# The first two merge gates of the delta-rule branch computed as one pair of column blocks, with seven block products in three of eight k-tile pairs

## The chip, the cores and the metric

The kernel runs on one core of one Trainium2 chip. The metric is the device time in microseconds, as a median over repeated runs. TensorE (PE) does the matrix products, PEld is its weight load, VectorE is DVE, ScalarE is ACT, GpSimd is POOL, and SP issues the loads of the weights.

## What is computed

One layer of a hybrid decoder trunk, in float32, for 256 tokens of width 2048:

```python
xn = _rmsnorm(h, norm_mix_g[i])
z = xn @ w_in[i]
zm, zr, zs, zg = jnp.split(z, IN_SPLIT, axis=-1)
...
g_m, g_r, g_s = jnp.split(jax.nn.sigmoid(zg), N_BRANCH, axis=-1)
mixed = (g_m * (y_m @ w_up_m[i]) + g_r * (y_r @ w_up_r[i]) + g_s * (y_s @ w_up_s[i]))
h = h + mixed @ w_out[i]
hn = _rmsnorm(h, norm_ffn_g[i])
h = h + (jax.nn.silu(hn @ ffn_w_gate[i]) * (hn @ ffn_w_up[i])) @ ffn_w_down[i]
hp = _rmsnorm(h, norm_ple_g[i])
h = h + (p[i] @ ple_w_proj[i]) * jax.nn.sigmoid(hp @ ple_w_gate[i])
return _rmsnorm(h, final_norm_g)
```

`y_r` is the delta-rule branch (RWKV-7), `g_r` its merge gate: a product of the 256 x 2048 activations with 2048 of the columns of `w_in`.

## The kernel before, in words

Every float32 operand of a large product is split into a high and a low part (`hi`, `lo`), and a product is three matmuls: high by high, low by high, high by low (`mm2`, lines 142 to 148). The tokens are two halves of 128 (`TS`). The activations stand in `ahi` and `alo`, 16 k-tiles of 128 each. The weights lie in HBM as chunks of 1 MB, in the order in which they are used. A chunk holds four tiles of 128 x 512. SP loads it into one of three `raw` buffers; ACT casts it into `whi` and DVE subtracts to get `wlo` (lines 131 and 132 in `chunk`), two tiles at a time, with three buffers each for `whi` and `wlo`.

`gemm_tm` multiplies 16 k-tiles with a block of 512 columns: four chunks, 96 matmuls of 512 columns, into two PSUM banks, one for each half of the tokens. PSUM has eight banks here, in two pools of four: `mm` (through `pmm()`) for the large products and `sm` (through `psm()`) for everything else.

`gemm_pair` does two blocks of 512 columns at once, in eight steps over pairs of k-tiles. It takes all four `mm` banks. An ordinary step is a chunk with four tiles and eight block products, 24 matmuls. A step of `SEVEN` is a Strassen-Winograd step: four sums of weight tiles (`seven`: two by POOL at lines 241 and 245, two by DVE), seven tiles to split, seven block products, 21 matmuls. Four of its seven products go to banks of `sm`, which the pair holds from the first such step to the last:

```python
if u == by7[0]:
    for q in (1, 7, 5, 6):
        M[q] = psm("M%d" % q)
(b11, b21), (b22, t3), (t1, t2_), (t4_,) = seven(pool)
...
prods([(1, A(u, 0, 0), b11)], end)
prods([(2, A(u, 0, 1), b21)], last)
prods([(3, S(u, 3), b22)], last)
prods([(7, S(u, 2), t3)], end)
```

Before the change it is used in the feed-forward part alone, with `ORDER = (3, 4, 0, 5, 1, 6, 2, 7)` and `SEVEN = (0, 1, 2)` for the gate and up blocks.

The order of instructions on each engine is made by a planner when the program is built: it takes what it expects to be ready, by priority, which is the order in the text, except for what stands under `tc.high_priority()`. So large products fill PE while the chain of the delta rule goes on. That chain stands in the text ahead of the gates of S5 and of the delta rule: `rw_chunk(0)` to `rw_chunk(3)`, then `rw_norm`. All its matmuls write `sm` banks. `rw_chunk` writes `pu` and `py` (lines 1130 and 1136), copies `pu` to `Up`, multiplies it into `px` (line 1148), copies that to `UV`, and finishes `py` (line 1136). `rw_norm` normalises `Yr` (DVE, ACT, and a power on POOL at line 1179), makes the bonus term in two banks `pq` (line 1185), and transposes `Yr` into two banks `pt` (line 1192). Then come the S5 gates and up blocks, the four delta-rule gates `z_gate("r", n)`, and the four up blocks of `y_r`.

Of the kernel before, what the change touches and what calls it, by code (L numbers as in the profile page):

```python
# [37 lines left out]
ORDER = (3, 4, 0, 5, 1, 6, 2, 7)  # L38
SEVEN = (0, 1, 2)

DORDER = tuple(range(22))
DSEVEN = (5, 8, 11, 14, 17)
# [35 lines left out]
def trunk(ctx: ExitStack, tc: tile.TileContext, xT, x, pT, wall, vecs, csts, s5b, s5c, gfin, out, dbg=None):  # L78
# [78 lines left out]
    TS = [slice(t * 128, (t + 1) * 128) for t in range(2)]  # L157
# [32 lines left out]
    def split(hi, lo, src, gain=None):  # L190

        if gain is None:
            nc.scalar.copy(out=hi, in_=src)  # L193
            nc.vector.tensor_tensor(out=lo, in0=src, in1=hi.bitcast(F32), op=ALU.subtract)  # L194
        else:
            nc.scalar.activation(out=hi, in_=src, func=AF.Identity if not isinstance(gain, float) else AF.Copy, scale=gain)
            nc.vector.scalar_tensor_tensor(out=lo, in0=src, scalar=gain, in1=hi.bitcast(F32), op0=ALU.mult, op1=ALU.subtract)
# [14 lines left out]
        tt(sf[:, 2], a[:, 0, TS[0]], a[:, 0, TS[1]], ALU.subtract)  # L212
        tt(sf[:, 3], a[:, 1, TS[0]], sf[:, 1], ALU.subtract)

    def sums_of(hi, lo, u, pool, tag="s"):

        af = t2("af").rearrange("p (a t) -> p a t", a=2)
        sf = t2("sf").rearrange("p (a t) -> p a t", a=4)
        tt(af, hi[:, 2 * u:2 * u + 2, :].bitcast(F32), lo[:, 2 * u:2 * u + 2, :].bitcast(F32), ALU.add)
        sums(sf, af)  # L220
        r = tuple(pool.tile([128, 4, 128], F32R, name=q + "%d" % u, tag="%s%s%d" % (tag, q, u)) for q in ("h", "l"))
        split(*r, sf)
        return r

    def tiled(r):

# [3 lines left out]
        split(hi, lo, r)  # L230
        return [(hi[:, q], lo[:, q]) for q in range(n)]

    def seven(pool):

        if not loaded:
            load()
        raw, _ = loaded.pop(0)
        with tc.high_priority():
            ts_ = pool.tile([128, 3, 512], F32, name="tsum", tag="tsum", bufs=2)
            out_ = [tiled(raw[:, 0:2])]  # L240
            nc.gpsimd.tensor_tensor(out=ts_[:, 0], in0=raw[:, 3], in1=raw[:, 0], op=ALU.subtract)  # L241
            tt(raw[:, 3], raw[:, 2], raw[:, 3], ALU.subtract)
            out_.append(tiled(raw[:, 2:4]))
            tt(ts_[:, 1], raw[:, 3], raw[:, 0], ALU.add)
            nc.gpsimd.tensor_tensor(out=ts_[:, 2], in0=raw[:, 1], in1=ts_[:, 1], op=ALU.subtract)
            out_ += [tiled(ts_[:, 0:2]), tiled(ts_[:, 2:3])]
        return out_
# [5 lines left out]
        while late:  # L253
            late.pop(0)()

    def gemm_pair(A, S, order, by7, pool, prep=None, onto=None):

        M = {q: pmm() for q in (2, 4, 3, 8)}
        done, res = set(), None

        def prods(ops, last):

            n_ = {q: max(i for i, o in enumerate(ops) if o[0] == q) for q in {o[0] for o in ops}}
            for part in range(2):
                for i, (q, a, w) in enumerate(ops):
                    mm2(M[q], *a, *w, part, q not in done, last and part == 1 and i == n_[q], True)
                    if part == 0:
                        done.add(q)

        for i, u in enumerate(order):  # L270
            if i == 2:
                run_late()
            last = u == order[-1]
            if prep is not None:
                prep(u)
            if u in by7:
                if u == by7[0]:
                    for q in (1, 7, 5, 6):
                        M[q] = psm("M%d" % q)
                (b11, b21), (b22, t3), (t1, t2_), (t4_,) = seven(pool)  # L280
                end = u == by7[-1]
                prods([(1, A(u, 0, 0), b11)], end)
                prods([(2, A(u, 0, 1), b21)], last)
                prods([(3, S(u, 3), b22)], last)
                prods([(7, S(u, 2), t3)], end)
                prods([(5, S(u, 0), t1)], end)
                prods([(6, S(u, 1), t2_)], end)
                prods([(4, A(u, 1, 1), t4_)], last)
                if end:

                    with tc.high_priority():
                        m1, u2, u3, u4, v4 = (t2(q) for q in ("m1s", "u2", "u3", "u4", "v4"))
                        nc.scalar.copy(out=m1, in_=M[1])
                        tt(u2, M[6], m1, ALU.add)
                        tt(u3, M[7], u2, ALU.add)
                        tt(u4, M[5], u2, ALU.add)
                        tt(v4, M[5], u3, ALU.add)
                    res = (m1, u3, u4, v4)
                    if onto is not None:
                        for o, r in zip(onto, res):  # L300
# [30 lines left out]
    def tt(o, a, b, op):  # L331
        nc.vector.tensor_tensor(out=o, in0=a, in1=b, op=op)
# [32 lines left out]
    ahi = act.tile([128, NKT, T], F32R, name="ahi", tag="ahi")  # L365
# [115 lines left out]
    G = {}  # L481
# [362 lines left out]
    mixed, gates = {}, {}  # L844

    def z_gate(key, n):
        ps = gemm_tm(xh, xl, NKT)
        with tc.high_priority():
            for t in range(2):
                g_ = t2("gate")  # L850
                act_fn(g_, ps[t], AF.Tanh, scale=hrs0[:, t:t + 1])
                gates[key, t, n] = g_

    def up(key, n, hi, lo, nkt, first):
        ps = gemm_tm(hi, lo, nkt)
        with tc.high_priority():
            for t in range(2):
                g_ = gates.pop((key, t, n))
                stt(g_, g_, 1.0, ps[t], ALU.add, ALU.mult)
                if first:  # L860
                    mixed[t, n] = g_
                else:
                    tt(mixed[t, n], mixed[t, n], g_, ALU.add)
# [387 lines left out]
    for n in range(4):  # L1251
        z_gate("s", n)
        up("s", n, lambda k: G["ysh"][:, k, :], lambda k: G["ysl"][:, k, :], 4, False)
    for n in range(4):
        z_gate("r", n)
    mT = {}
    for n in range(4):
# [53 lines left out]
    gu = gu_stack.enter_context(tc.tile_pool(name="gu", bufs=1))  # L1311
    hh, hl = hT

    SF = {u: sums_of(hh, hl, u, gu) for u in SEVEN}

    def A(u, t, k):
        return hh[:, 2 * u + k, TS[t]], hl[:, 2 * u + k, TS[t]]

    for b in range(11):
        c11, c21, c12, c22 = gemm_pair(A, lambda u, i: tuple(q[:, i, :] for q in SF[u]), ORDER, SEVEN, hid_p)  # L1320

        def swiglu(b=b, c11=c11, c21=c21, c12=c12, c22=c22):
            sg = []
            for t, (g_, u_) in enumerate(((c11, c12), (c21, c22))):
                s_ = t2("sg")
                act_fn(s_, g_, AF.Silu, scale=rs1[:, t:t + 1])
                stt(s_, u_, rs1[:, t:t + 1], s_, ALU.mult, ALU.mult)
                sg.append(s_)
            for q in range(4):
                pt = psm()  # L1330
                for t in range(2):
                    nc.tensor.transpose(pt[:, t * 128:(t + 1) * 128], sg[t][:, q * 128:(q + 1) * 128], ident)  # L1332
                nc.scalar.copy(out=hid[:, 4 * b + q, :], in_=pt[:, 0:T])
        late.append(swiglu)
# [24 lines left out]

    for n in (0, 2):  # L1360
        gemm_pair(lambda u, t, k: tuple(q[:, k, TS[t]] for q in dv["a"]), lambda u, i: tuple(q[:, i, :] for q in dv["s"]),
                  DORDER, DSEVEN, hid_p, down_prep, (h[0, n], h[1, n], h[0, n + 1], h[1, n + 1]))
        late.append(lambda n=n: [h_block(m, hT2, "gple", ssq2) for m in (n, n + 1)])
        if n == 0:
            late.append(p_halves)
# [74 lines left out]
def layout(i):  # L1440
# [35 lines left out]
    def block(w):  # L1476
        k = w.shape[0]
        for c in range(k // 512):
            chunks.append(w[c * 512:(c + 1) * 512].reshape(4, 128, 512).transpose(1, 0, 2).reshape(128, 2048))

    def blocks(w):
        for n in range(w.shape[1] // 512):
            block(w[:, n * 512:(n + 1) * 512])

    block(w_in[:, 6088:6600])
    block(lora_c)
    blocks(w_in[:, 0:4096])
# [9 lines left out]
    for n in range(4):  # L1497
        block(w_in[:, 10696 + n * 512:10696 + (n + 1) * 512])
        block(a["w_up_s"][0][:, n * 512:(n + 1) * 512])
    blocks(w_in[:, 8648:10696])  # L1500
    blocks(a["w_up_r"][0])
    blocks(a["w_out"][0])

    def pair(l, r, order):

        l, r = (q.reshape(-1, 2, 128, 512) for q in (l, r))
        for u in order:
            chunks.append(np.stack([l[u, 0], l[u, 1], r[u, 1], r[u, 0]], axis=1).reshape(128, 2048))

    for n in range(11):  # L1510
        c = slice(n * 512, (n + 1) * 512)
# [50 lines left out]
```

## Time and profile before

| | |
|---|---|
| median of 3 runs | 1658.6 us (1657.91 to 1659.91) |
| the profiled execution | 1657.76 us |
| its span in the profile | 1655.9 us |
| PE busy | 1633.6 us (99%) |
| DVE busy | 1314.9 us (79%) |
| ACT busy | 912.9 us (55%) |
| POOL busy | 202.7 us (12%) |

The span runs from the first to the last instruction; 1.86 us of the profiled execution lie around it. A busy PE is a pipelined one: matmuls overlap, so that the distance from one to the next is shorter than the duration of one.

### The profile page before, as it was taken

The page shows a single profiled execution, that of the slowest core. Times are in us where ns is not written, and L with a number is a line of the kernel's source. Part 1 is how long each engine was busy: PE and PEld are TensorE (multiplying, and loading weights), DVE is VectorE, ACT ScalarE, POOL GpSimd, SP SyncE. Part 2 cuts the span into 40 slices and gives each one's busy share as a digit, 9 for nine tenths or more (in the row PEclk, how much of TensorE's full clock was granted, in tenths as well). Part 3 has the DMA queues.
Part 4 walks back from the last instruction along what each step waited for, and adds up shares of the span by engine and source line. Part 5 has one row for each costly group of instructions (what it writes and reads, how often), then busy time and mean ns, then how long its engine had stood idle before and what let it go on. Part 6 is the DMA issues. An engine that isn't in the chain of part 4 may idle for free. (4 is left out here: it accounts for less than half of the span.)

```text
span 1655.9 us, 23640 instructions
## 1 busy us (share of the span) xinstructions
PE 1633.6 (99%) x9225; PEld 1375.7 (83%) x9225; DVE 1314.9 (79%) x1672; ACT 912.9 (55%) x1174; POOL 202.7 (12%) x151
## 2 busy tenths in 40 slices
PE   8999999999999999999999999999999999999997
PEld 8999889987888878888887888888888888888886
DVE  6999776969988546565588889899888988888665
ACT  6465466555645443444556555555555566666554
POOL 1100100100000000000032222222222121011000
PEclk9999999999999999999999999999999999999999
DMA  9654545555454444555544555455555555555553
GB/s 364 198 171 174 174 153 177 196 187 182 175 181 156 149 156 155 189 196 193 203 175 181 204 203 194 191 192 189 201 204 203 189 193 203 198 199 196 226 189 116
DMA packets 49456, 313.70 MB, mean 189 GB/s; under 512 B 5824, under 2 KB 9152, under 8 KB 12736
## 3 DMA queue, kind: packets, MB, share of 16 engines
q1 hardware_dynamic: 43488, 304.59, 50.8%
q0 software_dynamic: 3840, 3.15, 1.0%
q10 hardware_dynamic: 2016, 4.46, 0.8%
q8 instruction: 72, 1.18, 0.3%
q14 instruction: 40, 0.33, 0.1%
HBM read 306.93 MB, written 2.10 MB: 187 GB/s over the span
## 5 line engine op out<-in xcount | busy, mean ns | idle before, releaser
L131 ACT CAST whi<-raw 128x1024 fp32r<-128x1024 f32 (+1 forms) x476 | 495.7, 1048 | 492.2 <-PE mm L146 336.5
L132 DVE TENSOR_TENSOR wlo<-raw,whi 128x1024 fp32r<-128x1024 f32 (+1 forms) x476 | 602.4, 1271 | 192.2 <-ACT whi L131 166.7
L146 PE MATMUL mm<-whi,alo 128*128 128x512 f32 x512 | 201.5, 394 | 0.0
L145 PE MATMUL mm<-whi,ahi 128*128 128x512 f32 x512 | 201.2, 393 | 0.0
L145 PE MATMUL mm<-whi,hhi 128*128 128x512 f32 x506 | 199.5, 394 | 0.5 <-ACT whi L193 0.2
L146 PE MATMUL mm<-whi,hlo 128*128 128x512 f32 x506 | 197.1, 390 | 0.0
L152 PE MATMUL mm<-ahi,whi 128*128 128x256 f32 x576 | 143.2, 286 | 7.4 <-ACT whi L131 7.4
L148 PE MATMUL mm<-wlo,hhi 128*128 128x512 f32 x506 | 146.3, 393 | 2.2 <-DVE wlo L194 2.0
L153 PE MATMUL mm<-alo,whi 128*128 128x256 f32 x576 | 142.7, 286 | 0.0
L148 PE MATMUL mm<-wlo,ahi 128*128 128x512 f32 x512 | 139.3, 393 | 0.0
L241 POOL TENSOR_TENSOR tsum<-raw 128x512 f32<-128x512 f32 x43 | 66.3, 1542 | 551.1 <-DMA raw<-in_wall 269.4
L193 ACT CAST whi<-raw 128x1024 fp32r<-128x1024 f32 x86 | 90.4, 1051 | 66.8 <-PE mm L146 52.7
L194 DVE TENSOR_TENSOR wlo<-raw,whi 128x1024 fp32r<-128x1024 f32 x86 | 119.1, 1405 | 6.9 <-PE mm L148 6.5
L152 PEld LDWEIGHTS mm<-ahi,whi 128*128 128x128 f32 x576 | 111.4, 194 | 8.3 <-ACT whi L131 7.4
L145 PEld LDWEIGHTS mm<-whi,hhi 128*128 128x128 f32 x506 | 95.1, 188 | 24.5 <-issue 3.9
L148 PEld LDWEIGHTS mm<-wlo,hhi 128*128 128x128 f32 x506 | 94.7, 188 | 24.0 <-DVE wlo L194 4.5
L145 PE MATMUL mm<-whi,dh 128*128 128x512 f32 x292 | 114.0, 392 | 0.0
L145 PEld LDWEIGHTS mm<-whi,ahi 128*128 128x128 f32 x512 | 96.2, 188 | 21.1 <-issue 1.2
L146 PEld LDWEIGHTS mm<-whi,alo 128*128 128x128 f32 x512 | 96.3, 188 | 20.9 <-issue 1.2
L146 PE MATMUL mm<-whi,dl 128*128 128x512 f32 x292 | 113.5, 390 | 0.0
L148 PEld LDWEIGHTS mm<-wlo,ahi 128*128 128x128 f32 x512 | 95.7, 188 | 20.5 <-issue 0.4
L153 PEld LDWEIGHTS mm<-alo,whi 128*128 128x128 f32 x576 | 111.4, 194 | 0.7 <-issue 0.4
(558 smaller groups left out, 2935.7 us busy)
## 6 DMA issues: line engine op xcount, KB each, us to landing
raw<-in_wall SPq DMA_DIRECT2D x283, 1024.0 KB, 4.8
xrow<-in_x SPq DMA_DIRECT2D x2, 1024.0 KB, 9.3
h<-in_x ACTq DMA_DIRECT2D x8, 256.0 KB, 3.1
xraw<-in_xT SPq DMA_DIRECT2D x3, 512.0 KB, 9.5
ub<-Bh POOLq DMA_DIRECT2D x16, 64.0 KB, 3.9
ub<-uh POOLq DMA_DIRECT2D x16, 64.0 KB, 3.8
gft<-in_gfin ACTq DMA_DIRECT2D x1, 1024.0 KB, 7.4
out_dram<-fin SPq DMA_DIRECT2D x4, 256.0 KB, 3.2
```

Source lines behind the costliest of these rows:

```text
L131: nc.scalar.copy(out=hi[:, q, :], in_=r)
L132: nc.vector.tensor_tensor(out=lo[:, q, :], in0=r, in1=hi[:, q, :].bitcast(F32), op=ALU.subtract)
L145: nc.tensor.matmul(ps, ah, wh, start=first, stop=False, skip_group_check=skip)
L146: nc.tensor.matmul(ps, al, wh, start=False, stop=False, skip_group_check=skip)
L148: nc.tensor.matmul(ps, ah, wl, start=False, stop=last, skip_group_check=skip)
L152: nc.tensor.matmul(ps, wh, ah, start=first, stop=False, skip_group_check=skip)
L153: nc.tensor.matmul(ps, wh, al, start=False, stop=False, skip_group_check=skip)
L193: nc.scalar.copy(out=hi, in_=src)
L194: nc.vector.tensor_tensor(out=lo, in0=src, in1=hi.bitcast(F32), op=ALU.subtract)
L241: nc.gpsimd.tensor_tensor(out=ts_[:, 0], in0=raw[:, 3], in1=raw[:, 0], op=ALU.subtract)
```

## The change

The blocks 0 and 1 of the delta-rule gates are computed by one `gemm_pair` (`z_gate2`); blocks 2 and 3 and the up blocks stay as they were. The sums of the activations that the three steps of seven products need (`sums_of`) are made for it too; they take the room of tiles that `rw_inverse` has left (`Dm`, `cm`, `X`, `XT`, `Y`, and one of the small buffers `b2`). The sums of weights take a buffer of `b8`, a pool of two, which `KR` and `UV` hold until the delta rule's last chunk. The weights of the two blocks are laid out in HBM by pairs. The tanh of the gates is taken from SBUF instead of PSUM. In the feed-forward part the same functions are called through other names.

```diff
-    def sums_of(hi, lo, u, pool, tag="s"):
+    def sums_of(hi, lo, room):
 
         af = t2("af").rearrange("p (a t) -> p a t", a=2)
         sf = t2("sf").rearrange("p (a t) -> p a t", a=4)
-        tt(af, hi[:, 2 * u:2 * u + 2, :].bitcast(F32), lo[:, 2 * u:2 * u + 2, :].bitcast(F32), ALU.add)
+        tt(af, hi.bitcast(F32), lo.bitcast(F32), ALU.add)
         sums(sf, af)
-        r = tuple(pool.tile([128, 4, 128], F32R, name=q + "%d" % u, tag="%s%s%d" % (tag, q, u)) for q in ("h", "l"))
-        split(*r, sf)
-        return r
+        split(*room, sf)
+        return room
+
+    def room_pb(i):
+        t_ = [G["pb"].tile([128, 512], F32, name="sx", tag=q) if q else t2("sx") for q in (("Dm", "cm"), ("X", "XT"), ("Y", None))[i]]
+        return tuple(q.rearrange("p (a t) -> p a t", a=4).bitcast(F32R) for q in t_)
+
+    def tsum_t8():
+        return t8("tsum").rearrange("p a t -> p (a t)")[:, 0:1536].rearrange("p (a t) -> p a t", a=3)
...
+    def act_of(hi, lo):
+        return lambda u, t, k: (hi[:, 2 * u + k, TS[t]], lo[:, 2 * u + k, TS[t]])
+
+    def sum_of(sf):
+        return lambda u, i: tuple(q[:, i, :] for q in sf[u])
...
+    def z_gate2(key, n, sf):
+
+        c4 = gemm_pair(act_of(ahi, alo), sum_of(sf), ORDER, SEVEN, tsum_t8)
+        with tc.high_priority():
+            for o, (t, m) in zip(c4, ((0, n), (1, n), (0, n + 1), (1, n + 1))):
+                act_fn(o, o, AF.Tanh, scale=hrs0[:, t:t + 1])
+                gates[key, t, m] = o
...
-    for n in range(4):
+    z_gate2("r", 0, {u: sums_of(ahi[:, 2 * u:2 * u + 2, :], alo[:, 2 * u:2 * u + 2, :], room_pb(u)) for u in SEVEN})
+    for n in (2, 3):
         z_gate("r", n)
...
-    blocks(w_in[:, 8648:10696])
+    pair(w_in[:, 8648:9160], w_in[:, 9160:9672], ORDER)
+    blocks(w_in[:, 9672:10696])
```

## Rows read from the trace of the kernel before

**Rows 1.** The page, busy time of PE: us, share of the span, instructions.
```profile
PE 1633.6 (99%) x9225; PEld 1375.7 (83%) x9225; DVE 1314.9 (79%) x1672; ACT 912.9 (55%) x1174; POOL 202.7 (12%) x151
```

**Rows 2.** What PE waited for: us in total, times, longest.
```profile
PE mm L152 <- ACT whi L131: 7.4, 1, 7.4
PE mm L148 <- DVE wlo L194: 2.0, 3, 1.5
```

**Rows 3.** Windows: us; busy PE, PEld, DVE, ACT, POOL; PEclk; DMA share; GB/s.
```profile
620.93:650.70 29.77, 29.77 (x219) 23.67 (x218) 17.34 (x21) 10.76 (x14) 0.00 (x0) 1.00 0.39 136
650.70:674.60 23.90, 23.90 (x161) 19.81 (x160) 16.00 (x15) 12.44 (x16) 3.79 (x1) 1.00 0.50 177
674.60:696.40 21.80, 21.80 (x98) 18.06 (x97) 9.80 (x8) 9.63 (x12) 0.00 (x0) 1.00 0.56 198
```

**Rows 4.** The bonus product's operand and matmuls by tile: ns, first and last start us.
```profile
L1185 PE MATMUL sm<-mur,ct x8: 379/380/484, 639.3 to 640.9; 128*128 128x256 f32 x8
...
L335 DVE SCALAR_TENSOR_TENSOR mur<-mur,vt,muk x4: 480/480/486, 500.8 to 502.0; 128x256 f32<-128x256 f32 x4
```

**Rows 5.** Timeline: the delta rule between its first two chunks: start us, us.
```profile
588.21 0.37 ACT L1165 COPY Yr<-sm 128x256 f32<-128x256 f32 x1 [2.34 <-PE sm L1136]
...
594.00 1.15 PE L1130 MATMUL sm<-ST,KR 64*64 64x64 f32 x32
```

**Rows 6.** An earlier case by tile: mLSTM scores, an S5 slice, mLSTM numerators.
```profile
L335 DVE SCALAR_TENSOR_TENSOR E<-sm,E x4: 552/558/558, 179.1 to 184.9; 128x384 f32<-128x384 f32 x4
...
L611 PE MATMUL sm<-ub x8: 280/283/366, 184.6 to 201.7; 96*128 96x256 f32 x8
...
L807 PE MATMUL sm<-vtm,E x2: 379/380/382, 201.8 to 202.0; 128*128 128x258 f32 x2
```

**Rows 7.** Timeline: the delta rule's last chunk and its norm, on four engines.
```profile
633.79 0.37 ACT L1144 COPY Up<-sm 128x256 f32<-128x256 f32 x1 [2.42 <-PE sm L1136]
...
638.68 0.68 PE L1148 MATMUL sm<-Up,NX 64*64 64x64 f32 x16
...
640.00 0.43 DVE L1150 COPY UV<-sm 64x256 f32<-64x256 f32 x1
...
644.19 0.33 PE L1136 MATMUL sm<-UV,GB 128*64 128x64 f32 x2
...
649.86 1.29 DVE L332 TENSOR_TENSOR bon<-sm,muv 128x512 f32<-128x512 f32 x2
...
652.19 1.22 DVE L132 TENSOR_TENSOR wlo<-raw,whi 128x1024 fp32r<-128x1024 f32 x1
...
653.72 3.79 POOL L1179 TENSOR_TENSOR grs<-st,nhalf 128x16 f32<-128x16 f32 x1 [135.10 <-ACT whi L131]
...
657.54 1.23 DVE L332 TENSOR_TENSOR Yr<-Yr,grs 128x1024 f32<-128x1024 f32 x1
...
663.17 2.08 PE L1192 MATMUL sm<-ct,Yr 64*64 64x64 f32 x64
```

**Rows 8.** Groups of the pairs in the feed-forward part, and one tile's first and last start.
```profile
L194 DVE TENSOR_TENSOR wlo<-raw,whi 128x1024 fp32r<-128x1024 f32 x86 | 119.1, 1405 | 6.9 <-PE mm L148 6.5
...
L194 DVE TENSOR_TENSOR wlo<-tsum,whi 128x1024 fp32r<-128x1024 f32 x86 | 90.1, 1057 | 26.0 <-PE mm L148 16.2 <-PE sm L1332 7.0 <-ACT whi L193 0.6
...
L332 DVE TENSOR_TENSOR raw<-raw 128x512 f32<-128x512 f32 x43 | 29.5, 686 | 26.0 <-POOL tsum L241 26.0
...
L332 DVE TENSOR_TENSOR m1s<-mm,m1s x11: 680/682/684, 877.5 to 1308.4; 128x512 f32<-128x512 f32 x11
```

**Rows 9.** Timeline: PE's first matmuls, after its wait at the start.
```profile
9.71 0.42 PE L152 MATMUL mm<-ahi,whi 128*128 128x256 f32 x1
9.92 0.41 PE L153 MATMUL mm<-alo,whi 128*128 128x256 f32 x1
...
10.45 0.28 PE L152 MATMUL mm<-ahi,whi 128*128 128x256 f32 x1
10.57 0.28 PE L153 MATMUL mm<-alo,whi 128*128 128x256 f32 x1
```

More of the change, by code (lines that the diff above doesn't have):

```diff
@@ L213, in sums, with room_of, tsum_of @@
         tt(sf[:, 3], a[:, 1, TS[0]], sf[:, 1], ALU.subtract)
-    def sums_of(hi, lo, u, pool, tag="s"):
+    def sums_of(hi, lo, room):
         af = t2("af").rearrange("p (a t) -> p a t", a=2)
         sf = t2("sf").rearrange("p (a t) -> p a t", a=4)
-        tt(af, hi[:, 2 * u:2 * u + 2, :].bitcast(F32), lo[:, 2 * u:2 * u + 2, :].bitcast(F32), ALU.add)
+        tt(af, hi.bitcast(F32), lo.bitcast(F32), ALU.add)
         sums(sf, af)
-        r = tuple(pool.tile([128, 4, 128], F32R, name=q + "%d" % u, tag="%s%s%d" % (tag, q, u)) for q in ("h", "l"))
-        split(*r, sf)
-        return r
+        split(*room, sf)
+        return room
+    def room_of(pool, name):
+        return tuple(pool.tile([128, 4, 128], F32R, name=name + q) for q in ("h", "l"))
+    def room_pb(i):
+        t_ = [G["pb"].tile([128, 512], F32, name="sx", tag=q) if q else t2("sx") for q in (("Dm", "cm"), ("X", "XT"), ("Y", None))[i]]
+        return tuple(q.rearrange("p (a t) -> p a t", a=4).bitcast(F32R) for q in t_)
+    def tsum_of(pool):
+        return lambda: pool.tile([128, 3, 512], F32, name="tsum", tag="tsum", bufs=2)
+    def tsum_t8():
+        return t8("tsum").rearrange("p a t -> p (a t)")[:, 0:1536].rearrange("p (a t) -> p a t", a=3)
     def tiled(r):
@@ L231, in tiled, with seven @@
         return [(hi[:, q], lo[:, q]) for q in range(n)]
-    def seven(pool):
+    def seven(room):
         if not loaded:
@@ L238, in seven @@
         with tc.high_priority():
-            ts_ = pool.tile([128, 3, 512], F32, name="tsum", tag="tsum", bufs=2)
+            ts_ = room()
             out_ = [tiled(raw[:, 0:2])]
@@ L254, in run_late, with gemm_pair @@
             late.pop(0)()
-    def gemm_pair(A, S, order, by7, pool, prep=None, onto=None):
+    def act_of(hi, lo):
+        return lambda u, t, k: (hi[:, 2 * u + k, TS[t]], lo[:, 2 * u + k, TS[t]])
+    def sum_of(sf):
+        return lambda u, i: tuple(q[:, i, :] for q in sf[u])
+    def gemm_pair(A, S, order, by7, room, prep=None, onto=None):
         M = {q: pmm() for q in (2, 4, 3, 8)}
@@ L279, in gemm_pair @@
                         M[q] = psm("M%d" % q)
-                (b11, b21), (b22, t3), (t1, t2_), (t4_,) = seven(pool)
+                (b11, b21), (b22, t3), (t1, t2_), (t4_,) = seven(room)
                 end = u == by7[-1]
@@ L1312, in trunk @@
     hh, hl = hT
-    SF = {u: sums_of(hh, hl, u, gu) for u in SEVEN}
-    def A(u, t, k):
-        return hh[:, 2 * u + k, TS[t]], hl[:, 2 * u + k, TS[t]]
+    SF = {u: sums_of(hh[:, 2 * u:2 * u + 2, :], hl[:, 2 * u:2 * u + 2, :], room_of(gu, "sf%d" % u)) for u in SEVEN}
     for b in range(11):
-        c11, c21, c12, c22 = gemm_pair(A, lambda u, i: tuple(q[:, i, :] for q in SF[u]), ORDER, SEVEN, hid_p)
+        c11, c21, c12, c22 = gemm_pair(act_of(hh, hl), sum_of(SF), ORDER, SEVEN, tsum_of(hid_p))
         def swiglu(b=b, c11=c11, c21=c21, c12=c12, c22=c22):
@@ L1361, in trunk @@
         gemm_pair(lambda u, t, k: tuple(q[:, k, TS[t]] for q in dv["a"]), lambda u, i: tuple(q[:, i, :] for q in dv["s"]),
-                  DORDER, DSEVEN, hid_p, down_prep, (h[0, n], h[1, n], h[0, n + 1], h[1, n + 1]))
+                  DORDER, DSEVEN, tsum_of(hid_p), down_prep, (h[0, n], h[1, n], h[0, n + 1], h[1, n + 1]))
         late.append(lambda n=n: [h_block(m, hT2, "gple", ssq2) for m in (n, n + 1)])
@@ L1483, in blocks, with pair @@
             block(w[:, n * 512:(n + 1) * 512])
+    def pair(l, r, order):
+        l, r = (q.reshape(-1, 2, 128, 512) for q in (l, r))
+        for u in order:
+            chunks.append(np.stack([l[u, 0], l[u, 1], r[u, 1], r[u, 0]], axis=1).reshape(128, 2048))
     block(w_in[:, 6088:6600])
@@ L1499, in layout @@
         block(a["w_up_s"][0][:, n * 512:(n + 1) * 512])
-    blocks(w_in[:, 8648:10696])
+    pair(w_in[:, 8648:9160], w_in[:, 9160:9672], ORDER)
+    blocks(w_in[:, 9672:10696])
     blocks(a["w_up_r"][0])
     blocks(a["w_out"][0])
[L1504 to L1508, printed above, removed]
     for n in range(11):
```

## The prediction

> **What bounds the kernel now.** I read the page's busy time first: PE is busy for 1633.6 of 1655.9 us [rows 1]. The list of waits tells what that is worth: PE waits 7.4 us once, at the start, and after that hardly at all, 2.0 us in three waits being the next entry [rows 2]. So a matmul less is time less, and a microsecond in which PE stands still is a microsecond more; nothing behind it can give it back.
>
> Next the windows around the change. The third block of the four gates (674.60 to 696.40) is undisturbed: 21.80 us for 96 matmuls, 0.227 us each [rows 3]. The first block takes 29.77 us and the second 23.90, since matmuls of the delta rule run between theirs: 8.0 and 2.1 us more than 21.8 [rows 3]. That is the point that matters: the gates are the filling of PE while the last chunks of the delta rule and its norm go on.
>
> Last the timelines of that chain, with one question: who gets the banks of `sm`? The bonus product's operand is finished by 502.5 us, but its matmuls run at 639.3 [rows 4], right behind the last chunk's `px`, which starts at 638.68 [rows 7]. Nor did it lack a bank: between 588.6 us, when a chunk's results are copied out, and 594.0, when the next chunk begins, the chunk's new state alone can hold one of the four [rows 5]. In the text it stands behind `px`. An earlier case looks the same: the numerators' first operand is finished by about 179.7, yet their first matmul runs at 201.8, right behind the S5 slice that stands ahead of them in the text and was late [rows 6]. I read both as one rule of this planner: a tile of a pool gets no buffer before all tiles that come ahead of it in the text have theirs, even if buffers are free.
>
> **The change part by part.** *Removed.* The pair has 5 x 24 + 3 x 21 = 183 matmuls in place of 192: nine times 0.227 = 2.0 us less on PE.
>
> *Moved behind the norm.* The pair's four products M1, M7, M5 and M6 go to `sm`. In the text they come behind `rw_norm`, whose last two banks are those of the transposes at line 1192. By the rule above M1 can't begin before these transposes have; they start at 663.17 [rows 7]. The old gates, in `mm` alone, knew no such tie. The pair reaches M1 far earlier. It starts at 620.93 and has before M1 two ordinary steps, 48 matmuls or 10.9 us, and then the products 2 and 3 of the first step of seven, 6 matmuls or 1.4 us. Nothing else can fill PE: `whi` and `wlo` have three buffers, the first holds the tile of product 1, the second and third those of products 7, 5 and 6, so neither the seventh tile nor the next step's get a place; the blocks 2 and 3 need `mm` banks, and the pair has all four. PE can do the delta rule's own matmuls, 8.0 + 2.1 = 10.1 us [rows 3]. In all 22.4 us of work until M1.
>
> When do the transposes come, with PE idle? From the chain as it was [rows 7], step by step. `Up` is copied by 634.16, `px` starts at 638.68: 4.5 us, because PE had its queue full of gate matmuls. Now PE runs out of ordinary work at about 635.5 (620.93 + 10.9, and some 3.7 of the delta rule's 8.0): 3.2 us earlier. `UV` is written by 640.43, and the next product starts at 644.19, 3.8 us later. Now it waits only for the bonus product, about 2 us behind `px`, which leaves 0.9 us: 2.8 us less. Then DVE put the bonus multiply and a weight split (1.29 us at 649.86, 1.22 us at 652.19) between the norm's steps, together some 2.2 us. The first is out of the way by then, the second has no buffer to write: 2.2 us less. The power on POOL, 3.79 us, stays. From the end of the last multiply, 658.77, to 663.17 are again 4.4 us of queue; now about 0.1: 4.3 less. Sum 12.5, so the transposes start at 650.7 and end, 2.08 us later, at 652.8. From 620.93 that is 31.9 us, less 22.4 of work: PE stands still for 9.5 us.
>
> Bounds of this wait, by the same rows: if the queue's delays stay as they were, it ends at 665.3 and is 22 us; if the bonus product runs later and M1 needs only the second bank's first transpose, it ends some 3 us earlier and is 6. I take 9.5, near the lower end, because the delays are those of a full queue and this one is empty.
>
> *The clock after the wait.* At the start, behind 7.4 us without a matmul [rows 2], those of 256 columns follow each other by 0.21 us up to 10.1 us and by 0.12 from then on [rows 9]: the first is 1.2 GHz, the second 2.4. About twelve ran at the lower level, 0.09 us more each: 1.1 us. A wait of this size with short matmuls in it is likely to bring the same, 1.2 us; between nothing and twice that. The Trainium skill, "TensorE: Matmul & The Clock Gate", section "Why this matters for your kernels", warns against idle gaps amid matmuls, since the clock falls back to half. No row of the middle of this kernel shows it, as PE never stands still there; without that rule the sum would be 1.2 us less.
>
> *Added.* Three steps of seven cost DVE, with the means of the feed-forward pairs [rows 8], 2 x 1.405 + 2 x 1.057 + 2 x 0.686 = 6.3 us each against 2 x 1.22 [rows 7] = 2.45. Eight additions of 0.69 us at the end come on top, and the sums of activations: for each step two instructions of 512 columns and four of 128, which I put at 0.3 us, under the 0.43 of one of 256 [rows 7]; 2.6 us a step, 7.8 in all. Once M1 opens, `whi` is empty of finished tiles and DVE has the rest to do with PE waiting for it; the pairs' own longest wait for a weight split is 1.5 us [rows 2]. I take 1.0 us, between nothing and 3. The sums of activations fit into the free time of DVE before (17.34 us busy of 29.77 in the first block [rows 3]) and into the wait itself. If that cover were gone they would cost their 7.8 us, which is in the DVE rival's case below. POOL is idle there but for the power [rows 7]; its sums of weights need the buffer of `KR`, free once the last chunk has read the state, before `Up`.
>
> *Nothing.* SP loads as many chunks of the same size. The tanh comes from SBUF, four instead of four. The names in the feed-forward part change no instruction. The norm's remaining steps end earlier than before, and the up blocks of `y_r` need them only behind the fourth gate, at some 718 us (696.4 + 21.8). The transition to block 2 costs what pairs cost in the feed-forward part: a pair there takes (1308.4 - 877.5) / 10 = 43.1 us [rows 8] for 41.5 us of large matmuls and the transposes between them.
>
> *Sum.* -2.0 + 9.5 + 1.2 + 1.0 = +9.7 us on the profiled execution's 1657.76 (span 1655.9 and 1.86 around it): 1667.5. That execution lies 0.84 us below the median of 1658.6, so the median comes to 1668.3.
>
> The Trainium skill, "Perfetto Trace Analysis", section "Optimizing Tensor Performance", asks that independent groups of matmuls rotate through banks, so that the evacuation of one runs beside the next. It speaks against this change, which takes all eight. By the rule a seam costs an evacuation, some 0.7 us for a bank; the feed-forward pairs, which do the same, show next to none at their seams [rows 2]. By the trace the harm is in who must come first, not in the number.
>
> **The rivals.** *The banks aren't tied.* If a free bank goes to whoever is ready, M1 begins at about 637 and the delta rule's norm waits for banks in its turn, with some 50 us in hand up to 718. Then only the saving is left, less small waits: 1656.6 to 1660, say 1657.5. For it speaks that the pairs run well in the feed-forward part [rows 8]; against it the two cases in which a ready tile with free banks waited [rows 4, 5, 6].
>
> *DVE becomes the bound*, banks free. Busy time in the first two blocks is 33.3 us [rows 3], 13.7 of it not the 16 splits of 1.22. The pair brings 5 x 2.45 + 3 x 6.3 + 8 x 0.69 = 36.7 and the sums of activations about 7.8: 58.2 us against PE's 41.5 + 10.1 = 51.6. If nothing of it moves out, +6.6 - 2.0 = +4.6: 1663.2. It decides from the point where less than 4.6 us of sums and norm find room outside. DVE's free time ahead of 620 speaks against it.
>
> *The wait isn't shortened*: the planner keeps the chain's pace, M1 at 665: -2.0 + 22 + 2 = +22, 1680.
>
> *Faster than before by more than the nine matmuls* has nothing in these rows that would pay for it.
>
> **How the numbers follow.** The wait behind the norm gets 0.68, untied banks 0.20, DVE 0.08, the long wait 0.04. The predicted time is the first's, 1668; its own range, from a wait of 6 to one of 16 us with the other bounds, is 1663 to 1676. The range for 8 in 10 reaches to the untied banks: 1657 to 1676. A measurement of this kernel can tell 0.2%, 3.3 us, from no change. Untied banks are nearly all within it (0.17), a little faster (0.03); the other three are slower, 0.80.
>
> **What would show it.** Right: in the profile after, PE idle between about 636 and 653 us but for the delta rule, M1's first matmul directly behind line 1192, the bonus product by 638, a dip of matmul speed thereafter, 183 matmuls in the pair, and all behind it shifted by some 10 us. Wrong: a matmul of M1 ahead of the transposes, which would take the largest term away; or waits of PE for `wlo` all through the pair, which would make it DVE.

## The result, and the profile after

The kernel after takes 1674.47 us (median of 4 runs, 1673.12 to 1675.23), the kernel before 1659.26 beside it (4 runs, 1657.91 to 1660.62): a ratio of 1.0089, with a 95% interval of 1.0077 to 1.0101. It is 15.2 us slower. The profiled execution of after took 1674.74 us, with a span of 1673.0.

First the page of after, busy time of the engines, and PE's row over the 40 slices of the span. It answers to [rows 1]; line numbers are those of the new kernel now (the norm's transposes are L1219, `px` is L1175, the bonus product L1212, the state's read L1157, the power L1206).

```profile
PE 1637.1 (98%) x9216; PEld 1377.7 (82%) x9216; DVE 1334.5 (80%) x1710; ACT 920.1 (55%) x1184; POOL 216.1 (13%) x157
...
PE   8999999999999996999999999999999999999997
```

Nine instructions fewer on PE, as the change says, and one slice of forty, the sixteenth, with a 6 in a row of nines. The list of what PE waited for, which answers to [rows 2], names it:

```profile
PE sm L1219 <- DVE Yr L351: 12.4, 1, 12.4
PE mm L152 <- ACT whi L131: 7.2, 1, 7.2
PE mm L148 <- DVE wlo L194: 3.1, 6, 1.5
```

The wait at the start is old. New is one wait of 12.4 us: PE stands before the transposes of the delta rule's norm, for the last multiply of `Yr` on DVE. PE's timeline around it:

```profile
636.76 1.15 PE L1157 MATMUL sm<-ST,KR 64*64 64x64 f32 x32
...
638.99 0.68 PE L1175 MATMUL sm<-Up,NX 64*64 64x64 f32 x16
639.61 1.99 PE L1212 MATMUL sm<-mur,ct 128*128 128x256 f32 x8
641.53 0.69 PE L1163 MATMUL sm<-UV,GB 128*64 128x64 f32 x16
...
643.34 0.50 PE L148 MATMUL mm<-wlo,sx 128*128 128x512 f32 x1 [0.46 <-DVE wlo L194]
656.23 3.68 PE L1219 MATMUL sm<-ct,Yr 64*64 64x64 f32 x64 [12.39 <-DVE Yr L351]
659.84 0.79 PE L145 MATMUL M<-whi,ahi 128*128 128x512 f32 x1
660.43 0.63 PE L146 MATMUL M<-whi,alo 128*128 128x512 f32 x1
```

The reader is to see three things. PE runs dry at 643.8. The first matmul of M1 (`M`, at 659.84) comes directly behind the transposes. And the same 64 transposes take 3.68 us where they took 2.08 [rows 7]. The windows tell why (busy PE, PEld, DVE, ACT, POOL, then the granted clock):

```profile
636.50:643.80 7.30, 6.80 (x94) 4.76 (x92) 4.27 (x5) 3.10 (x5) 4.04 (x3) 1.00 0.00 0
643.80:656.23 12.43, 0.04 (x1) 0.03 (x1) 9.15 (x11) 1.06 (x1) 5.74 (x3) 0.54 0.22 84
656.23:660.00 3.77, 3.77 (x65) 3.65 (x65) 0.00 (x0) 1.07 (x3) 0.00 (x0) 0.50 0.02 4
660.00:662.00 2.00, 2.00 (x5) 1.60 (x6) 1.00 (x1) 1.59 (x3) 0.00 (x0) 0.53 0.00 0
662.00:690.00 28.00, 28.00 (x124) 23.01 (x123) 24.54 (x26) 17.87 (x19) 3.94 (x2) 1.00 0.48 173
```

In the wait the granted clock falls to half, 1.2 GHz, and stays there through the transposes and the first five matmuls into `M` banks. While PE stands, DVE is busy for 9.15 of 12.43 us. With what, its timeline and then POOL's show:

```profile
640.88 0.43 DVE L1177 COPY UV<-sm 64x256 f32<-64x256 f32 x1
641.34 1.95 DVE L194 TENSOR_TENSOR wlo<-raw,whi 128x1024 fp32r<-128x1024 f32 x1
643.21 2.29 DVE L194 TENSOR_TENSOR wlo<-tsum,whi 128x1024 fp32r<-128x1024 f32 x1
645.42 1.21 DVE L1198 TENSOR_REDUCE st<-Yr 128x16 f32<-128x1024 f32 x1
646.55 0.68 DVE L351 TENSOR_TENSOR raw<-raw 128x512 f32<-128x512 f32 x1
...
647.33 0.69 DVE L351 TENSOR_TENSOR tsum<-raw 128x512 f32<-128x512 f32 x1
...
654.86 1.23 DVE L351 TENSOR_TENSOR Yr<-Yr,grs 128x1024 f32<-128x1024 f32 x1 [3.05 <-POOL grs L1206]
```

```profile
642.31 2.10 POOL L254 TENSOR_TENSOR tsum<-raw 128x512 f32<-128x512 f32 x1
...
651.88 2.94 POOL L1206 TENSOR_TENSOR grs<-st,nhalf 128x16 f32<-128x16 f32 x1 [1.60 <-DVE st L348]
```

`Yr` is complete at 642.63 (ACT's last copy, 642.26 and 0.37), but the norm's first sum on DVE starts at 645.42, behind two weight splits of the first step of seven, and two sums of weights of the second step follow amid the norm's own.

One stage carries nearly all of it. From the last start of a matmul of line 145 on the S5 tokens (`ysh`) to the first on those of the delta rule's up blocks (`yrh`), in before and then in after:

```profile
L145 PE MATMUL mm<-whi,ysh x32: 388/390/500, 508.0 to 618.7; 128*128 128x512 f32 x32
...
L145 PE MATMUL mm<-whi,yrh x32: 391/395/398, 717.9 to 740.5; 128*128 128x512 f32 x32
```

```profile
L145 PE MATMUL mm<-whi,ysh x32: 387/389/499, 510.5 to 621.2; 128*128 128x512 f32 x32
...
L145 PE MATMUL mm<-whi,yrh x32: 392/394/397, 734.2 to 756.8; 128*128 128x512 f32 x32
```

Before takes 618.7 to 717.9, 99.2 us; after takes 621.2 to 734.2, 113.0 us: 13.8 more. It adds up as -2.0 (nine matmuls) + 12.4 and 0.5 (waits) + 1.6 (transposes at half clock) + 1.0 (five matmuls 0.43 apart and not 0.227), which is 13.5, and 0.3 are left. The remaining 3.3 us between the two profiled spans lie elsewhere: 2.5 ahead of the stage, 0.8 behind it; the last section comes back to the 2.5.

### The profile page after: what moved, and what is told of

Same layout as the page of the kernel before. It is cut to its first block, busy times and chain, and to the rows that moved or that the text cites. A ratio compares the mean times of both kernels' runs of the same rounds, so it can differ in the third digit from the quotient of the medians.

```text
span 1673.0 us, 23695 instructions
## 1 busy us (share of the span) xinstructions
PE 1637.1 (98%) x9216; PEld 1377.7 (82%) x9216; DVE 1334.5 (80%) x1710; ACT 920.1 (55%) x1184; POOL 216.1 (13%) x157
## 5 line engine op out<-in xcount | busy, mean ns | idle before, releaser
L131 ACT CAST whi<-raw 128x1024 fp32r<-128x1024 f32 (+1 forms) x470 | 489.4, 1048 | 476.1 <-PE mm L146 316.2
L132 DVE TENSOR_TENSOR wlo<-raw,whi 128x1024 fp32r<-128x1024 f32 (+1 forms) x470 | 593.9, 1269 | 169.4 <-ACT whi L131 145.3
L145 PE MATMUL mm<-whi,ahi 128*128 128x512 f32 x494 | 194.7, 394 | 0.1
L146 PE MATMUL mm<-whi,alo 128*128 128x512 f32 x494 | 194.7, 394 | 0.0
L254 POOL TENSOR_TENSOR tsum<-raw 128x512 f32<-128x512 f32 x46 | 72.4, 1574 | 678.4 <-DMA raw<-in_wall 321.1
L148 PE MATMUL mm<-wlo,hhi 128*128 128x512 f32 x506 | 146.2, 392 | 2.6 <-DVE wlo L194 2.6
L148 PE MATMUL mm<-wlo,ahi 128*128 128x512 f32 x494 | 135.5, 393 | 0.0
L193 ACT CAST whi<-raw 128x1024 fp32r<-128x1024 f32 x92 | 96.6, 1052 | 69.3 <-PE mm L146 56.3
L194 DVE TENSOR_TENSOR wlo<-raw,whi 128x1024 fp32r<-128x1024 f32 x92 | 125.8, 1388 | 7.5 <-PE mm L148 7.1
L258 POOL TENSOR_TENSOR tsum<-raw,tsum 128x512 f32<-128x512 f32 x46 | 102.1, 2220 | 151.6 <-DVE tsum L351 146.4
L194 DVE TENSOR_TENSOR wlo<-tsum,whi 128x1024 fp32r<-128x1024 f32 x92 | 96.4, 1056 | 29.1 <-PE mm L148 17.8
L193 ACT CAST whi<-tsum 128x1024 fp32r<-128x1024 f32 x92 | 76.2, 837 | 77.0 <-PE mm L146 52.9
L148 PEld LDWEIGHTS mm<-wlo,hhi 128*128 128x128 f32 x506 | 94.6, 188 | 24.3 <-DVE wlo L194 4.9
## 6 DMA issues: line engine op xcount, KB each, us to landing
xraw<-in_xT SPq DMA_DIRECT2D x3, 512.0 KB, 10.9
```

Of the source, the lines that this page charges most:

```text
L131: nc.scalar.copy(out=hi[:, q, :], in_=r)
L132: nc.vector.tensor_tensor(out=lo[:, q, :], in0=r, in1=hi[:, q, :].bitcast(F32), op=ALU.subtract)
L145: nc.tensor.matmul(ps, ah, wh, start=first, stop=False, skip_group_check=skip)
L146: nc.tensor.matmul(ps, al, wh, start=False, stop=False, skip_group_check=skip)
L148: nc.tensor.matmul(ps, ah, wl, start=False, stop=last, skip_group_check=skip)
```

## The experiments

The theory after the result: M1 waits for the transposes, since `sm` banks are given in text order, and the wait was longer than forecast because the pair's own preparation for the steps of seven (sums and splits on DVE and POOL) lies in the norm's chain. The rivals: the banks aren't tied and DVE alone is late; the norm's chain is that long by itself; the saving of nine matmuls isn't there.

Each run is given with its time and its ratio to the kernel before on the same chip (1659.91 us beside the first four, 1659.98 beside the next three, 1660.19 beside the last three), and with the stage from `ysh` to `yrh` as above, which is read from one profiled execution each. Where the order of the blocks or of the steps changes, the weights in HBM are laid out in the new order.

| run | median us | ratio [95%] | stage us |
|---|---|---|---|
| before, beside after | 1659.26 | | 99.2 |
| after | 1674.47 | 1.0089 [1.0077, 1.0101] | 113.0 |
| norm behind the pair in the text | 1663.07 | 1.0019 [1.0010, 1.0027] | 102.6 |
| pair of the last two gates | 1660.68 | 1.0005 [0.9996, 1.0014] | 100.1 |
| ordinary steps first | 1672.02 | 1.0076 [1.0060, 1.0091] | 112.3 |
| second step of seven one step later | 1673.99 | 1.0084 [1.0070, 1.0098] | 113.0 |
| last two gates, sums early | 1659.06 | 0.9995 [0.9986, 1.0004] | 99.0 |
| wait filled with matmuls | 1671.91 | 1.0072 [1.0058, 1.0086] | 110.3 |
| preparation without priority | 1673.64 | 1.0081 [1.0066, 1.0096] | 112.8 |
| after, no sums of weights | 1669.29 | 1.0055 [1.0043, 1.0068] | 109.6 |
| norm behind, no sums of weights | 1657.84 | 0.9985 [0.9977, 0.9994] | 97.4 |
| last two gates, no sums of weights | 1657.82 | 0.9984 [0.9975, 0.9993] | 97.4 |

**1. The norm behind the pair in the text.** The instructions are the same; `rw_norm` asks for its banks later.

```diff
-    rw_norm()
     ...
     z_gate2("r", 0, ...)
+    rw_norm()
```

> The norm of the delta rule (rw_norm) stands behind the pair in the text; nothing else differs from the changed kernel. If M1 waits because its bank comes behind the transposes' banks in the text (the tie), it gets a bank at once: PE waits under 1 us in all inside the pair, the clock doesn't fall there, the norm runs beside the gates 2 and 3, and the time is 1659.3 - 2.0 + 0.5 = some 1657.5 us (1656 to 1660). If the wait is DVE's load (DVE as the bound of this stage), it stays in another place: the steps of seven wait for wlo, some 5 to 7 us, 1662 to 1664 us.

1663.07 us: 11.4 less than after. PE's timeline has M1 directly behind `px`, with nothing to wait for, and no wait at the transposes; another wait has come:

```profile
638.10 0.68 PE L1175 MATMUL sm<-Up,NX 64*64 64x64 f32 x16
638.71 0.50 PE L145 MATMUL M<-whi,ahi 128*128 128x512 f32 x1
...
640.47 0.68 PE L1163 MATMUL sm<-UV,GB 128*64 128x64 f32 x14 [0.53 <-DVE UV L1177]
...
644.68 0.73 PE L148 MATMUL M<-wlo,sx 128*128 128x512 f32 x2 [0.57 <-DVE wlo L194]
...
656.27 0.60 PE L145 MATMUL mm<-whi,ahi 128*128 128x512 f32 x1 [1.95 <-ACT whi L193]
```

The tie is shown: only the place of the norm in the text changed, and the first matmul of M1 came 21 us earlier and ahead of the transposes. That the banks are what ties them can be seen in after: product 3, which stands behind M1 in the text but writes an `mm` bank, runs ahead of the transposes (L148 at 643.34), while M1, whose first tile was split by 634.04, runs behind them. The time, though, lies in the rival's range (1662 to 1664) and not in that of the tie (1656 to 1660), and the stage is 102.6 us and not 97.2 (99.2 less 2.0). The three waits are 3.05 us, and only 0.57 of them are for `wlo`. The windows around the last of them, in the same columns as above:

```profile
650.00:655.00 5.00, 4.33 (x19) 3.19 (x17) 5.00 (x5) 2.36 (x3) 5.00 (x1) 1.00 0.60 210
655.00:660.00 5.00, 3.73 (x9) 2.93 (x10) 3.59 (x5) 3.46 (x4) 2.17 (x3) 0.66 0.58 210
```

Ahead of that wait DVE and POOL are busy for all of 5 us; behind it the clock is at 0.66. So a part of the DVE rival is there, hidden behind the tie.

**2. The pair made of the last two gates.** Blocks 0 and 1 are single again; 2 and 3 are the pair, long after the norm.

```diff
-    z_gate2("r", 0, {u: sums_of(...) for u in SEVEN})
-    for n in (2, 3):
+    for n in (0, 1):
         z_gate("r", n)
+    z_gate2("r", 2, {u: sums_of(...) for u in SEVEN})
```

> The pair is made of the gates 2 and 3 instead of 0 and 1, so that it begins at about 664 us, when the norm's transposes are done. Tie: no wait for a bank, PE waits under 1 us in the pair, 1657.5 us (1656 to 1659.5). DVE as the bound: the pair has 44.5 us of DVE work (36.7 and the sums) against 41.5 of PE, so 2 to 4 us of waits for wlo: 1659.5 to 1661.5 us.

1660.68 us, no different from before; the stage is 100.1 us. Away from the norm the pair costs nearly nothing, but the nine matmuls aren't seen either, and the time is again in the rival's range (1659.5 to 1661.5). PE waits twice for a weight split, 0.76 and 1.23 us:

```profile
692.75 0.73 PE L148 MATMUL M<-wlo,sx 128*128 128x512 f32 x2 [0.76 <-DVE wlo L194]
695.63 0.50 PE L148 MATMUL mm<-wlo,ahi 128*128 128x512 f32 x1 [1.23 <-DVE wlo L194]
```

**3. The ordinary steps first.** More work is put ahead of M1: four ordinary steps and not two.

```diff
+GORDER = (3, 4, 5, 6, 0, 1, 2, 7)
-        c4 = gemm_pair(act_of(ahi, alo), sum_of(sf), ORDER, SEVEN, tsum_t8)
+        c4 = gemm_pair(act_of(ahi, alo), sum_of(sf), GORDER, SEVEN, tsum_t8)
```

> The pair of gates 0 and 1 does four ordinary steps ahead of its first step of seven (order 3, 4, 5, 6, 0, 1, 2, 7). Tie: PE reaches M1 at about 655 us instead of 638, while the norm's transposes are done at 660 to 663: a wait of 3 to 8 us, less of a fall of the clock, 1661 to 1667 us. DVE as the bound: no wait at M1, but three steps of seven on end need 6.3 us of DVE each against 4.8 of PE: 3 to 5 us of waits for wlo inside them, 1660 to 1662 us.

1672.02 us, above what both expected: 48 matmuls, 10.9 us, went ahead of M1, and the wait fell by only 3.5 us:

```profile
641.99 0.68 PE L1176 MATMUL sm<-Up,NX 64*64 64x64 f32 x16
...
661.67 3.68 PE L1220 MATMUL sm<-ct,Yr 64*64 64x64 f32 x64 [8.94 <-DVE Yr L352]
665.28 0.79 PE L146 MATMUL M<-whi,ahi 128*128 128x512 f32 x1
```

`px` starts 3.0 us later than in after (638.99) and the transposes 5.4 later, though the stage began 1.7 earlier (619.5 against 621.2). The delta rule's matmuls stand in PE's queue behind the gates again, so that what is put ahead of M1 delays the chain on which M1 waits.

**4. The second step of seven one step later.** The order is 3, 4, 0, 5, 6, 1, 2, 7 (same edit, `GORDER` only).

> Order 3, 4, 0, 5, 6, 1, 2, 7: the second step of seven comes one step later, so that its chunk isn't loaded yet when PE waits and DVE and POOL do not prepare it between the norm's steps. Tie with a chain that DVE lengthens: M1 waits for the transposes as before, but the norm's steps on DVE lose 1.4 us of sums and some of the slow splits beside POOL: the wait is 1.5 to 3 us shorter, 1671.5 to 1673 us. If the chain's length has nothing to do with the second step: 1674.5 us, as the changed kernel.

1673.99 us, and the wait is unchanged. DVE's timeline shows a gain and its loss:

```profile
643.35 1.21 DVE L195 TENSOR_TENSOR wlo<-tsum,whi 128x1024 fp32r<-128x1024 f32 x1
644.48 1.21 DVE L1199 TENSOR_REDUCE st<-Yr 128x16 f32<-128x1024 f32 x1
...
653.94 2.29 DVE L352 TENSOR_TENSOR Yr<-Yr,grs 128x1024 f32<-128x1024 f32 x1 [2.84 <-POOL grs L1207]
```

```profile
653.89 1.25 POOL L259 TENSOR_TENSOR tsum<-raw,tsum 128x512 f32<-128x512 f32 x1
```

The split takes 1.21 us in place of 2.29, since POOL's first sum for the second step has moved away, and the norm starts 0.9 us earlier. But the second step's other sum on POOL now runs from 653.89 to 655.14, and the last multiply of `Yr`, from 653.94, takes 2.29 us in place of 1.23. This order moved the cost and didn't tell the theories apart.

**5. The last two gates, with their sums early.** As 2, but the sums of activations stand ahead of gates 0 and 1 in the text.

```diff
+    sfr = {u: sums_of(...) for u in SEVEN}
     for n in (0, 1):
         z_gate("r", n)
+    z_gate2("r", 2, sfr)
```

> The pair of gates 2 and 3 again, with the sums of activations made two blocks earlier in the text, ahead of the gates 0 and 1. If the 2.0 us that PE waited for wlo inside that pair came from these sums, which DVE made right ahead of the first step of seven, the waits in the pair go below 0.7 us and the time is 1.5 us under that of the pair without this: some 1659 us beside a kernel before of 1659.9, that is, a ratio of 0.9990 to 1.0000. If the steps of seven alone fill DVE: waits as before, 1660.7 us.

1659.06 us, a ratio of 0.9995: the best of the versions that form all the sums, and not to be told from before. The pair's waits are 0.3 and 0.4 us, the stage 99.0. The sums of activations ahead of the first step of seven were what made most of run 2's waits. What is left is seen at three matmuls with a `wlo` operand:

```profile
691.80 0.73 PE L148 MATMUL M<-wlo,sx 128*128 128x512 f32 x2 [0.31 <-DVE wlo L194]
...
693.50 0.50 PE L148 MATMUL mm<-wlo,ahi 128*128 128x512 f32 x1
...
705.89 1.20 PE L148 MATMUL mm<-wlo,ahi 128*128 128x512 f32 x4 [0.41 <-DVE wlo L132]
```

The list of waits counts only from the end of the matmul before (0.39 us long), but the pace is one start in 0.227. By the starts around them these three places lose 0.6, 0.3 and 0.7 us, the second without a wait in the list.

**6. The wait filled with matmuls.** 58 matmuls into a bank that nobody uses stand behind the bonus product, so that PE doesn't stand still; they and ACT's copy of one column of their bank are work added, and nothing else changes.

```diff
+        jk = psm("junk")
+        jo = pb.tile([128, 1], F32, name="junko")
+        for i in range(58):
+            nc.tensor.matmul(jk, ahi[:, 0, TS[0]], ahi[:, 0:2, :], start=i == 0, stop=i == 57)
+        nc.scalar.copy(out=jo, in_=jk[:, 0:1])
```

> The changed kernel with 58 more matmuls of 512 columns (13.2 us at 0.227) into a bank of their own between the bonus product and the transposes in the text; their result is not used. They fill PE's wait and change nothing in its cause. If 2.6 us of the loss are matmuls at 1.2 GHz behind the wait: line 1219's transposes take 2.1 us instead of 3.7, the first products of M run at 0.23 us, and the time is 1671.5 to 1672.5 us. If the transposes are slow for another reason: 1674.5 us. If the added matmuls get in the chain's way in PE's queue: up to 4 us more.

1671.91 us, 2.6 less than after, with 58 matmuls more. The transposes start when they did, take 2.08 us again, and M1 runs at full speed behind them:

```profile
656.21 2.08 PE L1224 MATMUL sm<-ct,Yr 64*64 64x64 f32 x64
658.22 0.50 PE L145 MATMUL M<-whi,ahi 128*128 128x512 f32 x1
658.56 0.40 PE L146 MATMUL M<-whi,alo 128*128 128x512 f32 x1
```

The stage is 2.7 us shorter (110.3). That is the price of the clock, by itself.

**7. The preparation without priority.** The steps of seven of this pair lose their `tc.high_priority()`.

> The changed kernel, with the preparation of the pair's steps of seven at the text's priority instead of the high one, so that DVE and POOL take the norm's steps first. If the wait is longer than predicted because this preparation stands between the norm's steps: the transposes start 2 to 3 us earlier against the end of the chunk before, and PE's wait at them falls from 12.4 to some 9.5 us. The time falls by less, since the weights' preparation is late then: 1672 to 1675 us. If the norm's own chain sets it: 12.4 us as before.

1673.64 us, with the same wait of 12.4: DVE's instructions come in the same order as in after. Perhaps the planner expected the preparation to be ready first; no run shows it. Run 7 says nothing on the question, which is why the next runs take the work away.

**8 to 10. No sums of weights.** In three kernels (after, run 1, run 5) the steps of seven form no sums of weights, and the split tiles stand in as operands, so that the matmuls are as many as in the pair and their values are not the reference's.

```diff
+        if room is tsum_t8:
+            with tc.high_priority():
+                p_, q_ = tiled(raw[:, 0:2]), tiled(raw[:, 2:4])
+            return [p_, q_, p_, q_[0:1]]
```

> The pair stays where the change put it, but its three steps of seven form no sums of weights: no sums on POOL and DVE and two splits a step instead of four, with split weight tiles in the place of the sums as operands, so the seven products are not those of the reference. Matmuls, banks and their order in the text are as after the change. Theory (the preparation of the steps of seven on DVE and POOL stretches the norm's chain): the norm's first sum on DVE follows Yr at once, some 2.8 us earlier, the wait at the transposes falls from 12.4 to 9 or 10 us, and the time to 1670 to 1672. Rival (the chain was mis-sized in itself, and the preparation lies in its gaps): the wait stays at 12 or above, and the time at 1673 to 1675.

1669.29 us, 0.7 below the theory's range, with a wait of 9.3 us at the transposes. ACT's last copy of `Yr`, and DVE's first and last step of the norm:

```profile
646.87 0.37 ACT L1196 COPY Yr<-sm 128x256 f32<-128x256 f32 x1 [0.94 <-PE sm L1167]
```

```profile
647.46 1.21 DVE L1202 TENSOR_REDUCE st<-Yr 128x16 f32<-128x1024 f32 x1
...
655.99 1.23 DVE L355 TENSOR_TENSOR Yr<-Yr,grs 128x1024 f32<-128x1024 f32 x1 [3.20 <-POOL grs L1210]
```

From the last copy of `Yr` (647.24) to the end of its last multiply (657.22) the norm takes 9.98 us; after took 13.46 (642.63 to 656.09). The preparation adds 3.5 us to the chain. The wait itself is no clean measure here: with two splits a step in place of four the `whi` buffers come free sooner, so that an ordinary step runs ahead of M1, and the chain starts later behind it, as in run 3.

> The norm behind the pair in the text, as in the first experiment (1663.1), and no sums of weights in the pair's steps of seven, with split weight tiles in the place of the sums, so that these products are not those of the reference. Theory (what was left there was DVE and POOL late with the preparation, in waits of 1.95, 0.57 and 0.53 us and 1.8 us at the lower clock): these waits go, and the time is 1657 to 1659. Rival (the waits come from the delta rule's chain holding buffers and banks): they stay, and the time is 1661 to 1663.

1657.84 us, a ratio of 0.9985 [0.9977, 0.9994]. The stage is 97.4 us, and PE's timeline names no wait in it any more. What run 1 still lost, 5.2 us of the stage, was the preparation, in waits and in the clock behind them.

> The pair made of the last two gates with its sums of activations early, as in the fifth experiment (1659.1), and no sums of weights in its steps of seven, with split weight tiles in the place of the sums, so that these products are not those of the reference. Theory (what eats the nine matmuls there is the preparation on DVE and POOL): from the tokens of S5 to those of the delta rule's up blocks PE takes 97 to 97.5 us instead of 99.0, and the time is 1657 to 1658. Rival (the pair's matmuls lose it themselves, or the delta rule's do): 98.5 us and more, and 1658.5 to 1659.5.

1657.82 us, 0.9984 [0.9975, 0.9993], and again a stage of 97.4:

```profile
L145 PE MATMUL mm<-whi,ysh x32: 387/389/499, 510.2 to 620.9; 128*128 128x512 f32 x32
...
L145 PE MATMUL mm<-whi,yrh x32: 388/392/397, 718.3 to 740.8; 128*128 128x512 f32 x32
```

At either place the pair saves 1.8 us of the stage when its preparation is left out, and the preparation costs nearly as much as that even at the better place (99.0 against 97.4, 1.6 us). It is what run 5's three late splits lose, 0.6 + 0.3 + 0.7. How much of their lateness is DVE's own work and how much POOL's sums beside it stays open.

## Why the prediction was right, and where its sizes were off

The direction and the mechanism were right; the total fell 6.5 us short, 1668.0 against 1674.47, inside the range but near its end. (The upper end of the first case, 1676, isn't what its terms give: a wait of 16 us with the other upper bounds, 2.4 and 3, comes to 1678.)

**The nine matmuls, -2.0: right.** With the preparation taken away they show as 1.8 us of the stage in two kernels (runs 9 and 10).

**The tie of the banks: right.** M1 comes directly behind the transposes, and run 1 undoes it with one line moved. The rule that was read from the late bonus product [rows 4] and the late numerators [rows 6], text order and not readiness, held where it decided. The rival "the banks aren't tied" is out.

**The wait, forecast 9.5, measured 12.85 (12.39 + 0.46): the term that was mis-sized most.** Taken together, the delays of PE's queue went as forecast: `px` starts 0.05 us after `Up` is written (638.94), `UV` (641.31) meets its product at 641.53, the transposes start 0.14 after the last multiply. With the 2.5 us by which all of it lies later, `Yr` should have been complete at 642.5 (645.97 before, less 3.2 and 2.8) and was at 642.63. The step that failed is the one on DVE: "the second has no buffer to write: 2.2 us less". The old weight split was gone, but the splits and sums of the first two steps of seven took its place. The norm's first sum started 2.8 us after `Yr` was there, and 0.68 and 0.69 us of sums of weights lay between its steps; the power on POOL gave 0.85 back (2.94 where 3.79 was reckoned). From `Yr` to the end of its last multiply before took 12.8 us, so the forecast had 10.6; after took 13.46, 2.9 over. Run 8 shows the cause: without the sums this stretch is 9.98, so they cost 3.5, less what the power gave back. The rest of the 3.35 us that the wait was over is mostly the work until M1, 22.0 us where 22.4 was reckoned. The cost of these sums and splits stood in the prediction, but as a load on DVE under the heading of M1 open, not as a delay of the chain that opens M1.

The clock times that were named missed by the same cause and by the shift. The bonus product came at 639.61, not by 638: `px` and it came as soon as `Up` allowed, but `Up` itself was copied 4.8 us later than before (638.57 against 633.79). Of this 2.5 is the shift of all that lies ahead. The other 2.3 come from the chunk ahead of it: DVE copies its part of that chunk's `UV` at 626.44 where before it did at 621.62, behind the sums of activations (614.0 to 622.9) and one more of their splits (625.73). The prediction had put these sums into DVE's free time; they cost little here, for `Yr` was only 0.2 us late. PE was idle from 643.8 to 656.2, not from 636 to 653; the delta rule's matmuls lay ahead of the gap and not within it. The transposes came at 656.23 where 650.7 was forecast.

**The clock after the wait, 1.2: mis-sized, measured 2.6.** The sign was right and the estimate was taken from matmuls of 256 columns at the start. Here the first work behind the wait was the 64 transposes, 1.6 us slower, and then five matmuls of 512 columns, 1.0 us. Run 6 confirms the sum (2.6 of the median, 2.7 of the stage). The Trainium skill, "TensorE: Matmul & The Clock Gate", section "Why this matters for your kernels", says that idle gaps amid matmuls bring the clock down. After agrees in the middle of the kernel, with a granted clock of 0.50 behind 12.4 us. Run 1's fall comes behind a wait of 1.95 us, shorter than the gaps that this section speaks of; the measurement decides.

**Waits for splits once M1 is open, 1.0: nothing was found.** From M1 to the first `yrh` matmul of after, PE's timeline names no wait; the one split that was late in the pair, 0.46 us, lies ahead of the transposes. The bound below was nothing, and that is where it came out. The rival of DVE as the bound is not the story of this kernel, but run 1 shows it as what comes next when the tie is gone: 3.2 us over before, where that rival had +4.6 (its 13.7 us of other work on DVE are 13.8 by the rows, which changes nothing).

**The sum.** With the measured sizes the terms give -2.0 + 12.85 + 2.6 = 13.5 of the 13.8 us of the stage, where the forecast had 9.7. The median came out 15.2 us above that of before; the other 1.4 us are not in this stage, and no run names them with certainty. The 6.5 us that the total fell short are these 1.4, the 4.1 of the stage, 0.7 by which the median of before beside it was higher than the 1658.6 reckoned with, and 0.3 of rounding.

## What to carry to other kernels

Where a planner gives out buffers in the order of the text, sharing a pool with a chain that stands ahead means waiting for the last step of that chain, however many banks are free: compare the text order of allocations with the order in time before merging work into such a place. When that wait is sized, look for the new work's own preparation on the engines of the chain it waits for. A saving of nine matmuls out of 192 is worth 2 us only where the extra sums and splits find an idle DVE and POOL; here they cost nearly all of it even at the better place (1.6 of 1.8 us).

## What the runs showed of the hardware that was not expected

A wait of only 1.95 us in run 1, ahead of which PE had been busy without a break since 644.68, was followed by eight matmuls 0.43 us apart, at half clock, for 3.4 us (656.27 to 659.66). They took 1.6 us more than at 0.227, so that this wait cost some 3.6 us. It is not so behind every small wait: behind run 2's of 0.76 and 1.23 us the clock stayed at 1.00 and the matmuls went on 0.23 us apart.

DVE is slowed by POOL: the same split of 128 x 1024 takes 2.29 us while POOL makes a sum of 128 x 512 (642.31 to 644.41) and 1.21 us in run 4, where that sum is away; the multiply of `Yr` goes from 1.23 to 2.29 us in run 4, where a sum of POOL has come beside it. The times are those of taking turns: the split ends 1.09 us after POOL's sum (645.50), the multiply also 1.09 (656.23 after 655.14), nearly what each takes alone, 1.21 and 1.23. POOL loses too: the power takes 2.94 us while DVE is idle, in after and in run 8, and 3.79 in before, with splits of DVE beside it (653.49 and 656.20, 1.23 us each).

The 2.5 us ahead of the stage have a place but no cause: 1.7 of them are a fall of the granted clock without any wait of PE, behind eight matmuls with an operand of four partitions, in the window from 164 to 172 us of after (the other 0.8 lie ahead of these eight, which begin at 163.88 and not at 163.08):

```profile
164.00:168.00 4.00, 4.00 (x15) 3.02 (x16) 3.52 (x6) 1.03 (x1) 0.00 (x0) 0.87 0.44 145
168.00:172.00 4.00, 4.00 (x14) 3.01 (x13) 1.65 (x4) 1.61 (x2) 0.00 (x0) 0.71 0.28 117
```

In the profiled run of before the same stretch is granted 1.00. Runs 1, 3 and 8 are like it; runs 2, 4 to 7, 9 and 10 show the fall, with the same instructions there. This part of the kernel isn't touched by the change, and the lengths of the stage above don't contain it; why the clock falls there in some executions was not tried.
